# A hybrid encoder step: which queue issues the weight loads of the time mixing layer

## The chip, the cores and the metric

The kernel runs on one core of a Trainium2 chip. The metric is the device time of one execution in microseconds; the table below gives the median of the runs of the kernel before. Durations of single instructions, waits and transfers come from one profiled execution, whose own time stands beside its span. Names: PE is TensorE, PEld its weight loads, DVE VectorE, ACT ScalarE, POOL GpSimd, SP SyncE. SP, ACT and POOL can issue transfers (DMAs); an engine works through its own list of instructions in order, so an issue that has to wait holds all that stands behind it in that list.

## The reference

One step of an encoder with two layers and a width of 1024, for a prompt of 1024 rows and 8 samples of 16 rows. Layer 0 is an RWKV-7 time mixing and an FFN, layer 1 an attention over a band of chunks with shared keys and values, and an FFN. Every sub-layer is normalised and modulated by shift, scale and gate that come from a condition vector. Cut to what the change touches:

```python
mod = silu(c) @ w_ada[l] + b_ada[l]          # shift, scale, gate
h = rms_norm(x, norm_mix) * (1 + sc_m) + sh_m
xx = h_prev - h
xr, xw, xk, xv, xa, xg = (h + xx * mix[i] for i in range(6))
r, k, v = xr @ w_r, xk @ w_k, xv @ w_v
decay = exp(-exp(-softplus(-(w0 + tanh(xw @ w1) @ w2)) - 0.5))
a_gate = sigmoid(a0 + (xa @ a1) @ a2)
g = sigmoid(xg @ g1) @ g2
kk = l2_normalize(heads(k * k_k))
k = k * (1.0 + (a_gate - 1.0) * k_a)
y, state = wkv7_scan(r, decay, k, v, -kk, kk * a_gate, state)
out = (group_norm(y) + bonus(r, k, v)) * g @ w_o
x = x + gt_m * out
...                                          # FFN 0, keys/values, attention, FFN 1
```

All of it is float32. A product is worked out as three products of rounded halves: each weight is split into hi and lo (`split`: ACT copies hi in a rounded form, DVE subtracts to get lo), and PE runs hi x hi, hi x lo and lo x hi.

## The kernel before

The program has two parts. `layer0a` is the time mixing of layer 0; it ends near 1320 us. Behind it stand the FFN of layer 0, the shared keys and values, the attention and the second FFN, which end the program and which the change does not touch.

`layer0a` works on three blocks of 384 columns (`NB`, `TB`). `proj(b)` makes the projections of block b: normalisation (`proj_h`), the low-rank paths for decay, a and g (`proj_lora`, with `lora_weights`, `lora_in`, `lora_pairs` and an inner function `outputs`), then k (`proj_k`), r (`proj_r`) beside small inverses, and v. `windows` runs the recurrence over chunks of 128 columns, with many round trips through DRAM: tiles are written (`spill`, `save`, names sp_... and sf_...) and read back in another layout (rr<-sf_cs, ag<-sf_a, XL, BK, pa, yg). `outproj(b)` multiplies by w_o and adds to x. The code alternates the windows of block b-1 with the projections of block b; the windows of the last block alternate with `outproj(0)`, with units 4 to 11 of the modulation (`ada_steps`) and with `outproj(1)`; `outproj(2)` comes last, alone. From `tail_open` on there are two raw buffers for weights and one load of look-ahead in `ada_steps` (`fetch_ahead`); before that there are three raw buffers.

A weight unit is 128 x 1024 float32, 512 KB. `wunit` (L253) takes a raw buffer, loads it on SP (L256) and splits it into whi (ACT, L263) and wlo (DVE, L264). The modulation's weights are loaded on SP in `ada_steps` (L203) and used without a split; the low-rank weights in `lora_weights` (L378), `lora_pairs` (L412) and `outputs` (L605). The first sixteen modulation loads, for units 0 to 3, are made while `proj_h(0)` runs; nearly all other transfers of the first part are SP's too, a few are ACT's.

`proj_k` has two small jobs on POOL: for each strip it sets the first column of each group of the tile ext to one (L703), ACT fills the rest with exponentials (L704), and POOL copies the last column of each group into eend (L705), 32 of each in all. POOL has nothing else to do before the tail of the first part, where it forms the sums x<-x (L1257) of the FFN that follows.

The order on each engine is not written by hand. The framework takes the program's text, simulates it with costs for every instruction and orders each engine's list by that simulation (`schedule_with_timeline_sim=True`), so that a job on another engine can change the order on all of them. Completion of a transfer issued on SP or ACT is told by one of eight semaphores that are used in turn; POOL's transfers have eight of their own.

Of the kernel before, what the change touches and what calls it, by code (L numbers as in the profile page):

```python
# [141 lines left out]
class Trunk:  # L142
# [54 lines left out]
    def ada_steps(self, units, tag="aux", bufs=1, tile=None):  # L197

        nc = self.nc

        def load(u, i):
            w = (tile or self.rawtile)()
            nc.sync.dma_start(w[:, :1024], self.a["wada"][u, i])  # L203
            return w
        todo = [(u, i) for u in units for i in range(4)]
        ahead = None
        for u in units:
            ps = self.bank(tag, bufs)
            for i in range(4):
                w = ahead or load(*todo.pop(0))  # L210
                ahead = load(*todo.pop(0)) if todo and self.fetch_ahead else None
                c = slice(i // 2 * 256, i // 2 * 256 + 256)
                for q in range(4):
                    mm(nc, ps[32 * q:32 * q + 32, c], self.scT[:, i % 2 * 4 + q, :], w[:, q * 256:q * 256 + 256], i % 2 == 0, i % 2 == 1)
                if i < 3:
                    yield
            sb = (tile or self.rawtile)()[:, :512]
            nc.scalar.activation(sb, ps, AF.Copy)
            for j in range(4):
                mm(nc, ps[:, j * 16:(j + 1) * 16], sb[:, j * 128:(j + 1) * 128], self.C("qs"), True, True)  # L220
            pv = ps[:, 0:64].rearrange("p (j n) -> p j n", n=16)[:, :, 0:9]
            bo = PAR["bada"] + u * 4
            bv = self.par[:, bo:bo + 4].rearrange("p (j o) -> p j o", o=1).broadcast_to([128, 4, 9])
            nc.vector.tensor_tensor(self.mod[:, u * 4:u * 4 + 4, :], pv, bv, ALU.add)
            yield
# [24 lines left out]
    def halves(self, src):  # L250
        return [self.half(src[:, p * 512:(p + 1) * 512]) for p in range(2)]

    def wunit(self, wp, src, n=1024, rows=128):  # L253

        raw = self.rawtile()
        self.nc.sync.dma_start(raw[:rows, :n], src)  # L256
        hi = wp.tile([128, 1024], F32R, tag="whi", name=self.nm("whi"), bufs=self.nhi)
        lo = wp.tile([128, 1024], F32R, tag="wlo", name=self.nm("wlo"), bufs=self.nlo)
        self.split(hi[:rows, :n], lo[:rows, :n], raw[:rows, :n])
        return hi, lo  # L260
# [111 lines left out]
    def lora_weights(self, n):  # L372

        nc = self.nc
        mixes, w = self.LORA[n]
        c = 8 * w * len(mixes)
        raw, m = self.rawtile(), self.rawtile()
        nc.sync.dma_start(raw[:, :c], self.a[n])  # L378
        for j, i in enumerate(mixes):
            v = lambda t: t[:, :c].rearrange("p (k j w) -> p j k w", j=len(mixes), w=w)[:, j]  # L380
            nc.vector.tensor_tensor(v(m), v(raw), self.P(f"mix{i}").rearrange("p (k o) -> p k o", o=1).broadcast_to([128, 8, w]),
                                    ALU.mult)
        nc.vector.tensor_tensor(raw[:, :c], raw[:, :c], m[:, :c], ALU.subtract)
        self.lw[n] = []
        for t in (raw, m):
            dt = self.dp.tile([128, c], F32, name=self.nm("lw"))
            nc.scalar.dma_start(dt, t[:, :c])
            self.lw[n].append(dt)
        return raw, m
# [16 lines left out]
    def lora_pairs(self, n, c):  # L406

        if n in self.lw:
            raws = []
            for d in self.lw[n]:  # L410
                raws.append(self.rawtile())
                self.nc.sync.dma_start(raws[-1][:, :c], d)  # L412
        else:
            raws = self.lora_weights(n)
        W = []
# [97 lines left out]
    def proj(self, b):  # L513

        if b == 0:
            self.lw = {}
            ring = (f() for _ in range(2) for f in self.early)
            self.ada = self.ada_steps((0, 2, 1, 3), "acc", 2, lambda: next(ring))
            self.A0 = [self.cp.tile([128, 9], F32, name=f"A0_{f}") for f in range(8)]
            self.proj_h(0)  # L520
            self.x = self.hsplit()
            self.ada = self.ada_steps(range(4, 12))
        x, k = self.x, self.mixed(2, b)
# [39 lines left out]
    def proj_lora(self, b, hi, lo):  # L563
# [38 lines left out]

        def outputs(u, h, l, t):
            raw = self.rawtile()
            nc.sync.dma_start(raw, self.a["g2"][u])  # L605
            gh = pp.tile([128, 1024], F32R, tag="whi", name=self.nm("whi"), bufs=self.nhi)
            gl = pp.tile([128, 1024], F32R, tag="wlo", name=self.nm("wlo"), bufs=self.nlo)
            nc.scalar.activation(gh, raw, AF.Copy)
# [79 lines left out]
    def proj_k(self, b, hi, lo):  # L688
# [3 lines left out]
        for f in range(8):  # L692
# [7 lines left out]
            ext = self.pp.tile([128, 408], F32, tag="ext", name=self.nm("ext"), bufs=1)  # L700
            for s, sx, n, i in self.spans(b):
                ev = ext[:, sx].rearrange("p (g t) -> p g t", t=n + 1)
                nc.gpsimd.memset(ev[:, :, 0:1], 1.0)  # L703
                nc.scalar.activation(ev[:, :, 1:], iv[:, s].rearrange("p (g t) -> p g t", t=n), AF.Exp, scale=-KAPPA)  # L704
                nc.gpsimd.tensor_copy(self.eend[:, f, i:i + ev.shape[1]], ev[:, :, n])  # L705
            nc.scalar.activation(iv, iv, AF.Exp, scale=KAPPA)
            sq = self.ev("sq", self.nsq)
            kk = self.ev("kk")
# [465 lines left out]
    def layer0a(self, ctx):  # L1174
# [22 lines left out]
        cw.close()  # L1197
        for _ in self.outproj(2):
            pass
        ct.push(c1)  # L1200
        return ct.close

# [739 lines left out]
```

## Time and profile before

| what | value |
|---|---|
| median of 3 runs | 3872.93 us (3872.54 to 3875.93) |
| the profiled execution | 3860.7 us, span 3858.9 us |
| granted TensorE clock, mean | 0.939 of full speed |
| busy: PE, PEld | 3511.3 us (91%), 3098.6 us (80%) |
| busy: DVE, ACT, POOL | 2288.8 us (59%), 1570.8 us (41%), 570.9 us (15%) |
| moved by DMA | 552.31 MB, mean 143 GB/s |
| transfers issued on POOL | none in the trace |

How to read it: the span goes from the first instruction to the last. In the chain of work, each piece was released by the piece before it, so that its pieces add up to the span. A row of waits names who waited, for whom, the sum in us, the count and the longest. "SPq" is the list in which SP issues transfers; a transfer's name is destination<-source, with in_ for the program's inputs, and raw for the buffer of a weight unit. Numbers behind the names are left out in the profile's groups.

### The profile page before, as it was taken

How to read it: one execution, taken by the hardware profiler on the slowest of the kernel's cores; microseconds unless marked ns; L12 is line 12 of the kernel's file. 1: busy time of each engine (PE TensorE's matmuls, PEld its weight loads, DVE VectorE, ACT ScalarE, POOL GpSimd, SP SyncE). 2: the span in 40 equal slices, each digit the busy share in tenths (PEclk: the TensorE clock that was granted, in tenths of full speed). 3: DMA queues.
4: the chain of work that ended last, by engine and by line, in shares of the span. 5: the costliest groups of instructions: out<-in, count | busy, mean ns of one | idle time of the engine just before them, and what ended most of it. 6: DMA issues, size and time to landing. Idle time of an engine off the chain costs nothing.

```text
span 3858.9 us, 72261 instructions
## 1 busy us (share of the span) xinstructions
PE 3511.3 (91%) x28614; PEld 3098.6 (80%) x28614; DVE 2288.8 (59%) x4388; ACT 1570.8 (41%) x2966; POOL 570.9 (15%) x473
## 2 busy tenths in 40 slices
PE   5789899988899699999999899789889799999999
PEld 4677777777667589999887879677677699999998
DVE  4667666765445665555456742676775764554567
ACT  5555555544323433333311353565654533333310
POOL 0000000000000264454000100000000254554000
PEclk9887999898889789999999999899999899999999
DMA  5775676676765322222755113454555322222521
GB/s 207 232 230 167 196 214 174 180 217 182 202 195 165 132 73 75 76 72 95 270 179 183 70 60 99 137 149 145 147 189 174 119 77 77 72 75 93 170 86 69
DMA packets 429443, 552.31 MB, mean 143 GB/s; under 512 B 128432, under 2 KB 297520, under 8 KB 424624
## 3 DMA queue, kind: packets, MB, share of 16 engines
q1 hardware_dynamic: 374960, 528.80, 43.2%
q10 hardware_dynamic: 54144, 18.89, 2.2%
q8 instruction: 225, 3.69, 0.4%
q14 instruction: 114, 0.93, 0.1%
HBM read 413.42 MB, written 134.12 MB: 142 GB/s over the span
## 4 chain that ended last, share of the span: by engine, by line
PE 69%; DMA 9%; DVE 7%; ACT 5%; issue 2%; SPq 0%; POOL 0%; ACTq 0%; DVEq 0%; POOLq 0%
PE S L139 32%; PE PT L139 15%; PE acc L139 11%; PE st L139 3%; PE O L139 2%; PE G L139 2%; DVE h L264 1%; PE PT L1768 1%; PE aux L139 1%; DMA yg<-y 1%; PE Y L139 1%; ACT pts L1769 1%; DMA rr<-sf_cs 1%; DMA TT<-Z 1%; DMA raw<-in_wada 1%
## 5 line engine op out<-in xcount | busy, mean ns | idle before, releaser
L139 PE MATMUL S<-h,w 128*128 128x320 f32 (+1 forms) x4944 | 696.5, 299 | 20.6 <-DVE h L264 8.5
L139 PEld LDWEIGHTS S<-h,w 128*128 128x128 f32 x4944 | 674.6, 192 | 28.8 <-DVE h L264 13.5
L139 PE MATMUL acc<-mx,whi 128*128 128x384 f32 x1728 | 504.6, 370 | 56.1 <-ACT mx L263 18.3
L139 PE MATMUL S<-h,wh 128*128 128x320 f32 (+1 forms) x2844 | 527.5, 336 | 12.4 <-DVE h L1141 6.7
L139 PEld LDWEIGHTS S<-h,wh 128*128 128x128 f32 x2844 | 453.8, 188 | 67.8 <-issue 11.4
L139 PEld LDWEIGHTS acc<-mx,whi 128*128 128x128 f32 x1728 | 337.4, 204 | 87.2 <-ACT whi L263 21.6
L263 ACT ACTIVATE w<-rq 128x512 fp32r<-128x512 f32 x308 | 192.2, 629 | 501.7 <-PE S L139 201.8
L264 DVE TENSOR_TENSOR w<-rq,w 128x512 fp32r<-128x512 f32 x308 | 270.9, 883 | 201.2 <-ACT w L263 200.3
L139 PE MATMUL PT<-h,w 128*128 128x320 f32 (+1 forms) x2448 | 353.5, 299 | 15.0 <-ACT w L263 6.8
L139 PEld LDWEIGHTS PT<-h,w 128*128 128x128 f32 x2448 | 336.1, 191 | 18.5 <-ACT w L263 7.1
L139 PE MATMUL acc<-mx,wlo 128*128 128x384 f32 x864 | 316.2, 366 | 4.0 <-DVE wlo L264 4.0
L139 PE MATMUL PT<-h,wh 128*128 128x320 f32 (+1 forms) x1428 | 287.2, 344 | 11.2 <-DVE wh L264 3.9
L1327 POOL TENSOR_TENSOR t<-t,t 128x576 f32<-128x576 f32 (+1 forms) x132 | 215.1, 1630 | 415.7 <-ACT t L1334 292.8
L139 PEld LDWEIGHTS PT<-h,wh 128*128 128x128 f32 x1428 | 233.9, 190 | 42.5 <-issue 5.0
L264 DVE TENSOR_TENSOR wlo<-raw,whi 128x1024 fp32r<-128x1024 f32 x114 | 138.9, 1220 | 111.6 <-ACT whi L263 108.5
L139 PEld LDWEIGHTS acc<-mx,wlo 128*128 128x128 f32 x864 | 175.6, 203 | 13.3 <-DVE wlo L264 6.0
L263 ACT ACTIVATE whi<-raw 128x1024 fp32r<-128x1024 f32 x114 | 119.6, 1053 | 144.7 <-PE acc L139 79.4
L264 DVE TENSOR_TENSOR h<-h,h 128x1024 fp32r<-128x1024 f32 (+4 forms) x112 | 122.9, 1111 | 92.2 <-ACT h L263 75.7
L263 ACT ACTIVATE wh<-rq 128x512 fp32r<-128x512 f32 x124 | 74.8, 625 | 242.5 <-PE S L139 159.7
L263 ACT ACTIVATE h<-h 128x1024 fp32r<-128x1024 f32 (+4 forms) x112 | 103.2, 935 | 172.4 <-DMA h<-sd 112.2
L1327 DVE TENSOR_TENSOR t<-S,t 128x576 f32<-128x576 f32 (+1 forms) x116 | 86.4, 744 | 129.8 <-PE S L139 129.8
L1394 DVE TENSOR_TENSOR h<-h,S 128x640 f32<-128x640 f32 (+1 forms) x150 | 111.9, 750 | 78.8 <-PE S L139 78.6
(423 smaller groups left out, 5633.2 us busy)
## 6 DMA issues: line engine op xcount, KB each, us to landing
h<-in_wada SPq DMA_DIRECT2D x64, 512.0 KB, 6.4
rq<-in_wg SPq DMA_DIRECT2D x88, 256.0 KB, 2.6
rq<-in_wu SPq DMA_DIRECT2D x88, 256.0 KB, 2.6
rq<-in_wd SPq DMA_DIRECT2D x88, 256.0 KB, 2.9
raw<-in_wada SPq DMA_DIRECT2D x32, 512.0 KB, 4.3
kc<-in_ck SPq DMA_DIRECT2D x16, 1024.0 KB, 5.1
vc<-in_cv SPq DMA_DIRECT2D x16, 1024.0 KB, 7.3
sd<-t SPq DMA_DIRECT2D x88, 160.0 KB, 1.9
```

The source lines that it names most:

```text
L139: return nc.tensor.matmul(out, lhsT, rhs, start=start, stop=stop)
L263: self.nc.scalar.activation(hi, x, AF.Copy)
L264: self.nc.vector.tensor_tensor(lo, x, hi, ALU.subtract)
L1327: eng.tensor_tensor(out, x, y, ALU.add)
L1394: nc.vector.tensor_tensor(y, y, d, ALU.add)
L1768: nc.tensor.transpose(pt[:, j * 128:(j + 1) * 128], P[:, j * 128:(j + 1) * 128], self.C("ident"))
L1769: nc.scalar.activation(pts[:, 0:nk * 128], pt[:, 0:nk * 128], AF.Copy)
```

## The change

The change adds an attribute `wqueue` and a method `wload`. Where `wqueue` is None, `wload` issues on SP, as before; otherwise on the engine that it names. The five places named above use it. `wqueue` is set to GpSimd right after `proj_h(0)`, in the first block, and back to None behind `outproj(2)`. By this place, all 155 weight loads of the first part after the first sixteen are issued on POOL: the low-rank weights, w_k, w_r and w_v of all three blocks, modulation units 4 to 11 and w_o. Their number and buffers stay. The two small jobs of `proj_k` leave POOL: the memset goes to DVE, the copy of the last column to ACT.

```diff
--- before.py
+++ after.py
@@ -200,7 +200,7 @@
 
         def load(u, i):
             w = (tile or self.rawtile)()
-            nc.sync.dma_start(w[:, :1024], self.a["wada"][u, i])
+            self.wload(w[:, :1024], self.a["wada"][u, i])
             return w
         todo = [(u, i) for u in units for i in range(4)]
         ahead = None
@@ -250,10 +250,15 @@
     def halves(self, src):
         return [self.half(src[:, p * 512:(p + 1) * 512]) for p in range(2)]
 
+    wqueue = None
+
+    def wload(self, out, src):
+        (self.wqueue or self.nc.sync).dma_start(out, src)
+
     def wunit(self, wp, src, n=1024, rows=128):
 
         raw = self.rawtile()
-        self.nc.sync.dma_start(raw[:rows, :n], src)
+        self.wload(raw[:rows, :n], src)
         hi = wp.tile([128, 1024], F32R, tag="whi", name=self.nm("whi"), bufs=self.nhi)
         lo = wp.tile([128, 1024], F32R, tag="wlo", name=self.nm("wlo"), bufs=self.nlo)
         self.split(hi[:rows, :n], lo[:rows, :n], raw[:rows, :n])
@@ -375,7 +380,7 @@
         mixes, w = self.LORA[n]
         c = 8 * w * len(mixes)
         raw, m = self.rawtile(), self.rawtile()
-        nc.sync.dma_start(raw[:, :c], self.a[n])
+        self.wload(raw[:, :c], self.a[n])
         for j, i in enumerate(mixes):
             v = lambda t: t[:, :c].rearrange("p (k j w) -> p j k w", j=len(mixes), w=w)[:, j]
             nc.vector.tensor_tensor(v(m), v(raw), self.P(f"mix{i}").rearrange("p (k o) -> p k o", o=1).broadcast_to([128, 8, w]),
@@ -409,7 +414,7 @@
             raws = []
             for d in self.lw[n]:
                 raws.append(self.rawtile())
-                self.nc.sync.dma_start(raws[-1][:, :c], d)
+                self.wload(raws[-1][:, :c], d)
         else:
             raws = self.lora_weights(n)
         W = []
@@ -518,6 +523,7 @@
             self.ada = self.ada_steps((0, 2, 1, 3), "acc", 2, lambda: next(ring))
             self.A0 = [self.cp.tile([128, 9], F32, name=f"A0_{f}") for f in range(8)]
             self.proj_h(0)
+            self.wqueue = self.nc.gpsimd
             self.x = self.hsplit()
             self.ada = self.ada_steps(range(4, 12))
         x, k = self.x, self.mixed(2, b)
@@ -602,7 +608,7 @@
 
         def outputs(u, h, l, t):
             raw = self.rawtile()
-            nc.sync.dma_start(raw, self.a["g2"][u])
+            self.wload(raw, self.a["g2"][u])
             gh = pp.tile([128, 1024], F32R, tag="whi", name=self.nm("whi"), bufs=self.nhi)
             gl = pp.tile([128, 1024], F32R, tag="wlo", name=self.nm("wlo"), bufs=self.nlo)
             nc.scalar.activation(gh, raw, AF.Copy)
@@ -700,9 +706,9 @@
             ext = self.pp.tile([128, 408], F32, tag="ext", name=self.nm("ext"), bufs=1)
             for s, sx, n, i in self.spans(b):
                 ev = ext[:, sx].rearrange("p (g t) -> p g t", t=n + 1)
-                nc.gpsimd.memset(ev[:, :, 0:1], 1.0)
+                nc.vector.memset(ev[:, :, 0:1], 1.0)
                 nc.scalar.activation(ev[:, :, 1:], iv[:, s].rearrange("p (g t) -> p g t", t=n), AF.Exp, scale=-KAPPA)
-                nc.gpsimd.tensor_copy(self.eend[:, f, i:i + ev.shape[1]], ev[:, :, n])
+                nc.scalar.activation(self.eend[:, f, i:i + ev.shape[1]], ev[:, :, n], AF.Copy)
             nc.scalar.activation(iv, iv, AF.Exp, scale=KAPPA)
             sq = self.ev("sq", self.nsq)
             kk = self.ev("kk")
@@ -1197,6 +1203,7 @@
         cw.close()
         for _ in self.outproj(2):
             pass
+        self.wqueue = None
         ct.push(c1)
         return ct.close
 
```

What this does to the lists of the engines shows best at two places. The first is the start. ACT's list of before, from the copy BKT<-acc of a modulation unit on; lw are the prepared low-rank weights that are stored for the other blocks, raw_429 and raw_430 the two halves of wa1, whi their rounded parts, XL the copy of a modulation unit's sums for which PE waits:

```order
L218 ACTIVATE BKT_212<-acc_187 128x512
L331 ACT_TABLE_LOAD
L331 ACTIVATE rstd_178<-rstd_178 128x408
L332 ACTIVATE ntmp_180<-rstd_178 128x408
L387 DMA lw_437<-raw_430 128x1024
L387 DMA lw_435<-raw_429 128x1024
L263 ACTIVATE whi_439<-raw_429 128x1024
L263 ACTIVATE whi_443<-raw_430 128x1024
L1017 ACTIVATE UV_3279<-S_136 64x256
L1018 ACTIVATE UV_3279<-S_136 64x256
L218 ACTIVATE XL_244<-acc_219 128x512
```

ACT's list of the change from its fourth row on, where nacc and ntmp are the squares of hb, the first block's input:

```order
L174 ACTIVATE scT<-scT 128x256
L392 DMA lw_437<-raw_430 128x1024
L392 DMA lw_435<-raw_429 128x1024
L268 ACTIVATE whi_439<-raw_429 128x1024
L268 ACTIVATE whi_443<-raw_430 128x1024
L435 ACTIVATE nacc_153<-hb 128x408
L435 ACTIVATE ntmp_155<-hb 128x408
```

The stores and splits of wa1 have moved from behind the normalisation to ahead of it; XL now follows the stores of the next low-rank weight, g1a, and the two copies UV. On DVE the preparation of wa1 moves in the same way, ahead of the sums of the squares.

The second place is the tail, where `outproj(2)` loads its eight units of w_o; raw_13623 is the fifth, raw_13746 the eighth. SP's list of before (x<-e stores the block's result, rr<-in_x reloads x):

```order
L1169 DMA x_108<-e_2260_13493 128x384
L1166 DMA rr_13572<-in_x 128x384
L256 DMA raw_13623<-in_rw_o 128x1024
L1169 DMA x_108<-e_2267_13533 128x384
L1166 DMA rr_13613<-in_x 128x384
L256 DMA raw_13664<-in_rw_o 128x1024
L256 DMA raw_13705<-in_rw_o 128x1024
L1169 DMA x_108<-e_2274_13574 128x384
L1166 DMA rr_13654<-in_x 128x384
L256 DMA raw_13746<-in_rw_o 128x1024
```

POOL's list of the change from the fourth load of the same eight on; the TENSOR_TENSOR rows are the sums for the FFN:

```order
L256 DMA raw_13582<-in_rw_o 128x1024
L1264 ISA
L1264 TENSOR_TENSOR x_13812<-x_13812,x_13808 128x256
L1264 TENSOR_TENSOR x_13813<-x_13813,x_13809 128x256
L1264 TENSOR_TENSOR x_13808<-x_13808 128x256
L1264 TENSOR_TENSOR x_13809<-x_13809 128x256
L1264 TENSOR_TENSOR x_13808<-x_13808,x_13812 128x256
L256 DMA raw_13623<-in_rw_o 128x1024
L1264 TENSOR_TENSOR x_13809<-x_13809,x_13813 128x256
L1264 TENSOR_TENSOR x_13812<-x_13812,x_13808 128x256
L256 DMA raw_13664<-in_rw_o 128x1024
```

The fifth load has moved from SP, where it stood between stores and reloads, to behind five sums on POOL, and the sixth behind two more; the last two follow after the nine sums that come then. The stores and reloads on SP no longer stand behind loads that wait for a buffer.

## The prediction

> **What bounds the kernel now.** I read the page's chain first, to see who holds the end, then busy time by stages, then the waits of SP, ACT and PE inside the stage that the change touches. The last section of chain on the page, and the stages (columns: stretch, its length, busy us of PE, PEld, DVE, ACT and POOL with instruction counts, granted clock, DMA share, GB/s):
>
> ```profile
> PE 69%; DMA 9%; DVE 7%; ACT 5%; issue 2%; SPq 0%; POOL 0%; ACTq 0%; DVEq 0%; POOLq 0%
> ...
> 100.00:700.00 600.00, 525.00 (x5363) 442.82 (x5361) 404.01 (x860) 329.37 (x612) 6.26 (x35) 0.88 0.70 202
> ...
> 930.00:1190.00 260.00, 227.36 (x2463) 175.20 (x2463) 125.99 (x293) 79.80 (x149) 0.00 (x0) 0.86 0.71 199
> ...
> 1400.00:3859.00 2459.00, 2331.37 (x16805) 2130.80 (x16803) 1432.71 (x2583) 912.88 (x1730) 495.97 (x351) 0.98 0.36 117
> ```
>
> PE is the bound. From 1400 us on it works 2331 of 2459 us, and none of that code is touched, so the change can only move the point at which that part starts. In the first 1400 us PE is still busy 87% of the time (525.00 of 600, 227.36 of 260). What is to be had is the rest, 75 us in one stretch and 33 in the other, and it is shared by many short waits. POOL is empty there. SP, which issues nearly every transfer, is not: its longest waits between 60 and 1340 us (what waits, for whom: us in total, times, longest) and, from the same view, ACT's and PE's waits for transfers are
>
> ```profile
> SPq L256 <- DVE wlo L264: 144.3, 38, 23.0
> ...
> ACT rr L552 <- DMA rr<-sf_cs: 42.0, 18, 5.6
> ACT mx L263 <- DMA mr<-yg: 27.2, 11, 7.6
> ACT whi L263 <- DMA raw<-in_rw_o: 24.7, 6, 7.3
> ACT kp L713 <- DMA ag<-sf_a: 22.1, 11, 6.0
> ...
> PE aux L139 <- DMA raw<-in_wada: 7.5, 6, 2.0
> ```
>
> The first row is the case for the change: 38 times SP stood with a weight load whose raw buffer was still read by DVE's split, 144.3 us in all, and everything behind that load on SP stood too. The rows under it say who could profit and who could lose. The reloads (sf_cs, yg, sf_a) stay on SP and could come earlier; the weight loads that are themselves waited for (in_rw_o, in_wada) go to the new queue.
>
> **Part 1: what SP gets back.** A hold of SP costs only if what stands behind it is awaited. The chain has SPq at 0%, that is under half a per cent, 19.3 us of 3858.9. The three kinds of reload were awaited for 42.0 + 27.2 + 22.1 = 91.3 us in 40 waits, 2.3 us each, while one of them takes longer than that only to land (columns: KB, median us from issue to landing):
>
> ```profile
> raw<-in_rw_k SPq DMA_DIRECT2D x24, 512.0 KB, 3.9
> raw<-in_rw_r SPq DMA_DIRECT2D x24, 512.0 KB, 5.4
> ...
> rr<-sf_cs SPq DMA_DIRECT2D x48, 192.0 KB, 3.4
> ...
> ag<-sf_a SPq DMA_DIRECT2D x24, 192.0 KB, 2.9
> ...
> gl<-sp_g SPq DMA_DIRECT2D x18, 256.0 KB, 4.0
> ...
> yg<-y ACTq DMA_DIRECT2D x18, 256.0 KB, 4.7
> ```
>
> So most of a wait is flight (2.9 to 3.4 us), and the queue is the smaller part. SP's issue of a weight load lasts 0.33 us by its row in part 3, with the step to the next issue 0.42 (1281.79 to 1282.21). If one weight load stood ahead of half of the 40 reloads, 20 x 0.4 = **-8 us**. The ends: nothing, if the transfers that matter were ready late anyway; and -27 us, if the whole 19.3 us of SPq on the chain goes as well. I take -8, since the quoted chain has SPq at 0% and a reload's flight stays. The 155 weight loads also stop using the eight semaphores that SP's and ACT's transfers share in turn; I count that inside the -8.
>
> **Part 2: loads that are awaited.** The transfers of weights on the chain between 930 and 1190 us (start, us, what):
>
> ```profile
> 967.25 5.54 DMA raw<-in_rw_v
> 1005.25 6.38 DMA raw<-in_wada
> 1048.59 6.34 DMA raw<-in_rw_o
> 1065.97 5.40 DMA raw<-in_wada
> 1072.34 5.46 DMA raw<-in_wada
> 1113.64 4.38 DMA raw<-in_wada
> 1145.58 5.63 DMA raw<-in_rw_o
> ```
>
> Seven loads, 39.1 us. There are two raw buffers in this stage and one load of look-ahead, and each of these steps begins with a buffer coming free, not with SP coming free: no step of the chain that names SPq stands between. What POOL adds to such a load in time to issue or land, the end gets in full. The trace has no transfer issued on POOL at all, so I bound it. The low end is 0. The nearest row of another queue is the 256 KB yg<-y on ACT's, 4.7 us against 4.0 for the 256 KB gl<-sp_g on SP's: +0.7. [...] I take the nearest row: 7 x 0.7 = **+5 us**, range 0 to +17. In the blocks' first two thirds there are three raw buffers and loads run ahead, so there I count nothing; the six in_rw_o waits of ACT and six in_wada waits of PE above are all that the loads had.
>
> [...]
>
> **Part 3: the start and the tail.** The change sets the queue already after the first block's normalisation, so the first block's LoRA weights go to POOL too, which is free from the beginning. Now (start, us, engine, line, [idle before]):
>
> ```profile
> 14.93 0.54 ACT L430 ACTIVATE nacc<-hb 128x408 f32<-128x408 f32 x1 [8.71 <-DMA hb<-in_xg]
> ...
> 17.48 0.33 SPq L378 DMA_DIRECT2D raw<-in_wa  x1
> ...
> 36.43 2.00 ACT L263 ACTIVATE whi<-raw 128x1024 fp32r<-128x1024 f32 x2 [8.59 <-DVE raw L383]
> 37.52 2.36 DVE L264 TENSOR_TENSOR wlo<-raw,whi 128x1024 fp32r<-128x1024 f32 x2 [1.50 <-ACT whi L263]
> ...
> 39.19 0.60 ACT L218 ACTIVATE XL<-acc 128x512 f32<-128x512 f32 x1
> ...
> 39.84 1.89 PE L139 MATMUL acc<-cst,XL 128*128 128x16 f32 x8 [6.61 <-ACT XL L218]
> ```
>
> ACT stood 8.59 us for DVE's preparation of the raw wa1, and PE 6.61 us for the copy XL that ACT has behind it. In the changed order the two whi and wlo stand ahead of the squares of hb, in time in which ACT was idle (8.71 us before 14.93). XL then comes after two 0.4 us copies alone. Of the 6.61 us I take **-4**: the g1a preparation (two DVE operations) moves ahead of hb's scaling and takes about 2.4 us of it back, worked out from twice the 1.2 us that one of its kind takes in the 2.36 row. Ends: -6.6, and +6 if the first POOL load lands so late that the squares, now behind it on ACT, start after 14.93 us.
>
> In the tail POOL has work of its own, the Strassen sums of the next stage:
>
> ```profile
> 1281.79 0.33 SPq L256 DMA_DIRECT2D raw<-in_rw_o  x1
> 1282.21 0.38 SPq L1169 DMA_DIRECT2D x<-e  x1
> ...
> 1283.15 18.43 SPq L256 DMA_DIRECT2D raw<-in_rw_o  x2
> ...
> 1279.62 7.30 POOL L1257 TENSOR_TENSOR x<-x,x 128x256 f32<-128x256 f32 x2 [465.96 <-DVE h L264]
> 1286.88 1.43 POOL L1257 TENSOR_TENSOR x<-x 128x256 f32<-128x256 f32 x2
> 1288.27 5.43 POOL L1257 TENSOR_TENSOR x<-x,x 128x256 f32<-128x256 f32 x6
> ```
>
> The load of 1281.79 stands in the new order behind five of these sums, so it goes out when the fifth ends, some 0.9 us (5.43 / 6) after 1288.3: about 1289.2, 7.4 us later than now, and lands about 1293.6 instead of 1286.2. Now the pair behind it is split no sooner than PE wants it; the next row of the chain that names weights is the split of a later load:
>
> ```profile
> 1300.02 1.22 DVE wlo L264
> 1301.28 19.45 PE acc L139 x94
> ```
>
> So of 7.4 us later at most a part is seen. The same reordering frees SP, which stood 18.43 us over two loads. I take **+3**, from 0 to +7.4.
>
> **Part 4: the small jobs.** On POOL (min/median/max ns) they were
>
> ```profile
> L703 POOL MEMSET ext<- x32: 104/108/114, 1.7 to 811.0; 128x6 f32 x16, 128x4 f32 x8, 128x8 f32 x8
> ...
> L705 POOL COPY eend<-ext x32: 185/190/1533, 117.7 to 813.1; 128x6 f32<-128x6 f32 x16, 128x4 f32<-128x4 f32 x8, 128x8 f32<-128x8 f32 x8
> ...
> L918 ACT ACTIVATE p<-st 32x256 f32<-32x256 f32 x32 | 12.0, 375 | 14.0 <-PE st L139 13.3
> ```
>
> 32 memsets on DVE at about POOL's 0.11 us are 3.5 us of an engine that is two thirds busy; 32 copies on ACT, at most 375 ns each, are 12 us of one that is 55% busy (329.37 of 600). Each stands between two exponentials of the same strip. The slack of ACT hides most; I take a quarter, **+3**. Ends: 0 and +12.
>
> **The sum.** -8 + 5 - 4 + 3 + 3 = -1 us. The profiled execution took 3860.7 us, so 3859.7 in its terms. The median of the runs shown, 3872.93, is 12.2 us above it, and I carry the difference to it: **3872 us**. A measurement of this kernel can tell about 0.2% from no change, 7.7 us. The reordering of every engine's list, which follows from other queues and costs in the scheduler, has no term; I allow +-10 us for it, a tenth of the 108 us in which PE is idle in the two stretches above.
>
> **Rivals.** (a) **SP's holds matter more.** If the awaited reloads also lose the 19.3 us that the chain may have in SPq, part 1 is -27 and the sum -20: 3853 us. For it speaks the 144.3 us row; against it SPq 0%. Chance 0.34. (b) **The loads themselves are late**, which is slower. [...] It decides from about +1.9 us a load, since (7.7 + 1) / 7 = 1.2 above the 0.7 taken. [...] Chance 0.2. [...] (c) **The first POOL load is late at the start**: the +6 end of part 3 instead of -4, 3882 us. Chance 0.08. (d) **Nothing to see** is my forecast itself: gain and loss within 7.7 us, chance 0.38. The change touches more than it says (the first block too), so that it does nothing is no case.
>
> **How the numbers follow.** Of the forecast's 0.38, the reordering lets 0.02 fall on either side; of (a)'s 0.34 a tenth stays within 0.2%. That gives faster 0.36, same 0.37, slower 0.27. The range takes in (a) with half of the reordering, 3853 - 5 = 3848, and (b), 3892, with 2 us more: 3848 to 3894. The likeliest case's own range is 3865 to 3880.
>
> **What would show it.** Right: the SPq row with 144.3 us is gone; PE's 6.61 us before 39.84 has shrunk to some 2; the seven chain rows of weights are each 0.5 to 1 us longer. Part 1 is wrong if the 91.3 us of ACT's waits fall by more than 20 us, or rise. Part 2 is wrong if weights on the chain take 7 us or more, or if they appear before 900 us. The tail is wrong if PE's long run at 1301.28 starts over 7 us later against the stretch before it. The forecast falls if PE's idle time before 1400 us changes by more than 8 us.

## The result, and the profile after

The changed kernel takes 3900.53 us in the median (3896.77 to 3907.33) against 3873.03 us before (3872.54 to 3875.93): a ratio of 1.0057 on record, with a 95% interval of 1.0039 to 1.0075. It is slower: by 0.57%, 22 us, by that ratio, and by 27.5 us between the two medians. Run again beside other kernels it gave 1.0058 (1.0036 to 1.0080). The prediction, 3872 us with a range up to 3894, missed it.

The profiled execution took 3896.77 us. To see where the time went, each execution is cut where PE has done the same matrix work: at the start of the first block's k units, at the end of its v units, at the start of the w_o stage (outproj(0), modulation units 4 to 11, outproj(1)), at the end of outproj(2). Stage rows of before, cut there (columns as in the prediction's stage rows), and then of the changed kernel:

```profile
137.40:302.90 165.50, 136.43 (x1145) 118.97 (x1144) 110.23 (x224) 93.02 (x172) 2.50 (x12) 0.91 0.80 234
302.90:923.70 620.80, 560.20 (x6540) 464.97 (x6539) 411.07 (x902) 327.76 (x633) 9.17 (x49) 0.88 0.66 189
923.70:1316.00 392.30, 326.27 (x3325) 256.61 (x3322) 208.52 (x458) 130.71 (x247) 19.54 (x16) 0.85 0.62 180
1316.00:3858.90 2542.90, 2398.33 (x17173) 2190.24 (x17172) 1490.34 (x2684) 950.54 (x1802) 537.54 (x384) 0.97 0.35 117
```

```profile
135.30:319.00 183.70, 141.16 (x1173) 125.22 (x1174) 112.34 (x233) 91.34 (x174) 11.62 (x22) 0.85 0.74 216
319.00:941.60 622.60, 568.91 (x6532) 477.96 (x6520) 411.18 (x921) 332.32 (x661) 33.77 (x65) 0.85 0.66 187
941.60:1347.40 405.80, 336.40 (x3321) 260.60 (x3319) 210.14 (x459) 131.40 (x246) 48.95 (x72) 0.83 0.59 174
1347.40:3895.00 2547.60, 2407.20 (x17173) 2197.43 (x17172) 1495.33 (x2684) 949.27 (x1801) 541.97 (x384) 0.97 0.35 116
```

The first block's projections take 183.70 us for 165.50, the w_o stage 405.80 for 392.30. The long middle, where the loads have slack, takes 622.60 for 620.80, though all its loads have moved too. The rest differs by less than two profiles of one kernel do, as shown below. So there are two places, +18 and +13.5 us, and PE loses its time in them in two ways. In the first, PE's idle time grows by 13.5 us (165.50 - 136.43 = 29.1 to 183.70 - 141.16 = 42.5). In the second it grows by 3.4 us only (66.0 to 69.4); the other 10.1 us are PE being busy longer (326.27 to 336.40) on the same matrix work, at a granted clock of 0.83 for 0.85.

SP's second longest wait of before, then SP's longest waits between 60 and 1380 us in the changed kernel, and ACT's waits for w_o and for the three kinds of reload that the prediction added up:

```profile
SPq L1169 <- DVE e L1141: 31.7, 12, 5.8
```

```profile
SPq L1175 <- DVE e L1147: 87.7, 14, 17.8
SPq L545 <- ACT kp L604: 61.8, 12, 40.9
SPq L822 <- PE G L852: 43.6, 6, 15.5
SPq L1175 <- DVE e L1152: 43.4, 8, 19.5
SPq L545 <- DVE kp L724: 40.8, 10, 10.2
...
ACT rr L558 <- DMA rr<-sf_cs: 44.0, 17, 5.2
ACT mx L268 <- DMA mr<-yg: 39.7, 12, 8.7
ACT whi L268 <- DMA raw<-in_rw_o: 32.1, 7, 7.6
...
ACT kp L719 <- DMA ag<-sf_a: 23.0, 11, 5.6
```

The row of 144.3 us is gone, as the change means it to. In its place SP stands at stores: x<-e (L1175) 87.7 us where it was 31.7 (L1169), the save of kp (L545) 61.8 and 40.8. All of SP's waits together, from the first block's k units to the end of outproj(2), are 757 us before and 834 in the changed kernel. ACT's waits for the three kinds of reload sum to 44.0 + 39.7 + 23.0 = 106.7 us; they were 91.3. When both kernels were profiled again (before_again and after_again below), SP's waits were 758 and 828 us, and those for the reloads 92.5 and 91.5, the last from these rows:

```profile
ACT mx L268 <- DMA mr<-yg: 39.8, 13, 8.6
ACT rr L558 <- DMA rr<-sf_cs: 36.3, 15, 6.1
ACT whi L268 <- DMA raw<-in_rw_o: 32.8, 7, 7.4
...
ACT kp L719 <- DMA ag<-sf_a: 15.4, 7, 6.0
```

So SP stands longer than before, in both pairs of profiles, and the waits for reloads do not fall; whether they rise, two profiles do not tell.

At the start, POOL, ACT and PE read:

```profile
1.72 0.69 POOL L256 DMA_DIRECT2D raw<-in_wa  x1
...
11.91 7.17 ACTq L392 DMA_DIRECT2D lw<-raw  x2
19.12 2.00 ACT L268 ACTIVATE whi<-raw 128x1024 fp32r<-128x1024 f32 x2 [13.21 <-DMA YL<-in_wada]
21.04 0.53 ACT L435 ACTIVATE nacc<-hb 128x408 f32<-128x408 f32 x1
...
39.65 1.06 PE L139 MATMUL acc<-cst,XL 128*128 128x16 f32 x8 [2.18 <-ACT XL L218]
```

PE's wait for XL has shrunk from 6.61 to 2.18 us, but the matmul starts at 39.65 instead of 39.84: the store of wa1 held ACT's list for 7.17 us, and the squares of hb began at 21.04 instead of 14.93.

### The profile page after: what moved, and what is told of

It reads as the page before. It is cut to its first block, busy times and chain, and to the rows that moved or that the text cites. A ratio compares the mean times of both kernels' runs of the same rounds, so it can differ in the third digit from the quotient of the medians.

```text
span 3895.0 us, 72310 instructions
## 1 busy us (share of the span) xinstructions
PE 3540.6 (91%) x28614; PEld 3125.9 (80%) x28614; DVE 2297.2 (59%) x4420; ACT 1572.7 (40%) x2998; POOL 645.1 (17%) x564
## 3 DMA queue, kind: packets, MB, share of 16 engines
q0 software_dynamic: 21840, 79.31, 6.7%
## 4 chain that ended last, share of the span: by engine, by line
PE 70%; DMA 11%; DVE 9%; issue 5%; ACT 4%; SPq 1%; POOL 0%; ACTq 0%; DVEq 0%; POOLq 0%
PE S L139 32%; PE PT L139 15%; PE acc L139 13%; PE st L139 3%; PE O L139 2%; DVE h L269 1%; PE G L139 1%; PE PT L1775 1%; PE aux L139 1%; DMA sp_b<-ag 1%; DMA raw<-in_rw_o 1%; DMA h<-out_kT 1%; DMA yg<-y 1%; DMA rr<-sf_cs 1%; DMA BK<-sp_k 1%
## 5 line engine op out<-in xcount | busy, mean ns | idle before, releaser
L139 PE MATMUL acc<-mx,whi 128*128 128x384 f32 x1728 | 512.5, 376 | 68.5 <-ACT mx L268 22.1
L139 PE MATMUL S<-h,wh 128*128 128x320 f32 (+1 forms) x2844 | 528.4, 337 | 12.6 <-DVE h L1147 7.1
```

The source lines that it names most:

```text
L139: return nc.tensor.matmul(out, lhsT, rhs, start=start, stop=stop)
```

## Experiments

All ratios are against executions of the kernel before that ran beside the kernel tried. Theories: **Q**, a load freed from SP's list competes with the transfers that are awaited; **J**, the small jobs cost; **R**, any new order moves the time by chance.

**small_only, loads_only, from_block1, to_outproj.** The first is the kernel before with these two lines, the others are the changed kernel with one edit each.

```diff
 # small_only, in before
-                nc.gpsimd.memset(ev[:, :, 0:1], 1.0)
+                nc.vector.memset(ev[:, :, 0:1], 1.0)
-                nc.gpsimd.tensor_copy(self.eend[:, f, i:i + ev.shape[1]], ev[:, :, n])
+                nc.scalar.activation(self.eend[:, f, i:i + ev.shape[1]], ev[:, :, n], AF.Copy)
 # loads_only, in the changed kernel: the same two lines back
 # from_block1, in proj
-            self.wqueue = self.nc.gpsimd
+        if b == 1:
+            self.wqueue = self.nc.gpsimd
 # to_outproj, in layer0a
+        self.wqueue = None
         self.tail_open(ct)
```

> Only the two small jobs of proj_k leave POOL; every weight load stays on SP. Theory Q (queue: a weight load issued on POOL goes out as soon as its buffer is free, shares the 16 transfer engines with the stores and reloads that the next step awaits, PE idles, and the clock is halved for the window that follows): no change, within 6 us of before. Theory J (the memset and the copy now stand in proj_k's chain on DVE and ACT, which is where the changed kernel loses its first 14 us, between 137 and 222 us): 10 to 16 us slower than before. Theory R (any new order of the lists moves the PE's idle windows and so the clock, by some 15 us either way): anywhere from 15 us faster to 15 us slower.

> All 155 loads on POOL as in the changed kernel, but the memset and the copy stay on POOL, between the loads. Theory Q: as slow as the changed kernel, 3890 to 3910 us, since the loads still run beside SP's transfers. Theory J: 14 us faster than the changed kernel, about 3886, unless the loads wait behind the small jobs, which wait for DVE and ACT. Theory R: no relation to the two, 3860 to 3910.

> The changed kernel with the queue set only when the second block's projections begin: the first block's loads stay on SP, the small jobs stay on DVE and ACT. Theory Q: the 14 us lost between 137 and 222 us come back, the 13 us lost between 1080 and 1145 us stay: 3883 to 3890. Theory J: nothing comes back, 3895 to 3905. Theory R: no relation, 3860 to 3910.

> The changed kernel with SP issuing again from the stage with two raw buffers on (w_o and the modulation units 4 to 11). Theory Q: the 13 us lost between 1080 and 1145 us come back, the first 14 stay: 3884 to 3890, and the weights on the chain there take as long as before, 4.4 to 6.4 us. Theory J: the same, since the small jobs end at 813 us and leave this stage alone; it differs from Q in the first stage alone. Theory R: no relation, 3860 to 3910.

Measured: small_only 1.000 (0.998 to 1.002), loads_only 1.0105 (1.0076 to 1.0133), from_block1 1.0084 (1.0057 to 1.0111), to_outproj 0.9987 (0.9971 to 1.0004). The w_o stage lasts 395.10, 417.80, 411.00 and 382.50 us. Taking POOL out of that stage alone brings the whole loss back, though it also leaves the stage 10 us shorter than in before, where the same queue loads it; taking it out of the first block brings nothing, against Q's 14 us. The two places of the changed kernel are told apart by the first block's row: small_only and loads_only read

```profile
134.80:308.30 173.50, 138.41 (x1177) 120.36 (x1179) 110.70 (x230) 91.03 (x172) 0.00 (x0) 0.87 0.78 227
```

```profile
133.10:311.20 178.10, 138.86 (x1171) 122.20 (x1173) 110.46 (x224) 91.84 (x169) 14.25 (x33) 0.87 0.75 222
```

Of 165.50 us before, the small jobs alone make 173.50 and the loads alone 178.10, both 183.70. PE is idle there for 35.1 us with the jobs alone (173.50 - 138.41) and 29.1 before. The other profiles of this section sort this place further. Three profiles with neither the jobs nor the first block's loads moved have 165.50 to 166.40 us for it; five with the jobs moved and these loads and all stores on SP (small_only, from_block1, block12, outproj_only, outproj_act) 173.50 to 179.60; five with both moved (the change, after_again, to_outproj, block0_only, after_x1pool) 177.60 to 185.20. So the jobs take the larger part here, 8 to 14 us, and the loads some 7 more on average. Yet small_only as a whole is no slower, to within 0.2% or 8 us, so that this stage's loss does not show in full in its total. J falls as a price of the whole kernel: loads_only, with the jobs back on POOL, is slower than the change, not faster.

**outproj_only, block12, block0_only, before_again.** POOL in one stage each, in the changed kernel; and the kernel before once more.

```diff
 # outproj_only: not set in proj, but in layer0a
+        self.wqueue = self.nc.gpsimd
         self.tail_open(ct)
 # block12: from_block1 and to_outproj together
 # block0_only, in proj
+        if b == 1:
+            self.wqueue = None
         x, k = self.x, self.mixed(2, b)
```

> Loads on POOL only in the stage with two raw buffers (w_o and modulation units 4 to 11, 56 loads); the three blocks' projections load on SP; small jobs on DVE and ACT. Theory B (the loss is made in this stage, where loads are awaited and w_o and the modulation share two buffers and now one POOL list): 15 to 35 us slower than before, with the stretch from the first w_o load to the last outproj(1) step 10 to 25 us longer. Theory A (the loss is made in the projections, by loads that compete with stores): within 6 us of before. Theory R (each new order lands at random within 15 us): no relation.

> Loads on POOL in the second and third blocks' projections alone (w_k, w_r, w_v and the stored low-rank weights of two blocks); first block and the stage of w_o on SP. Theory B: within 8 us of before, either way. Theory A: 15 to 30 us slower than before, since from_block1, which shares this part, was the furthest behind when that stage began. Theory R: no relation.

> Loads on POOL in the first block alone, up to the end of its low-rank part and of its k, r and v units (the queue goes back to SP when the second block's projections begin). Theory B: within 8 us of before. Theory A: the 14 us lost between 137 and 222 us show in full, 10 to 16 us slower. Theory R: no relation.

> The kernel before itself, once more, with its own profile: what two profiles of the same lists differ by. All theories: a ratio of 1.000. If the number of half-clock windows before 1400 us is fixed by the order of the lists it stays near 127; if it is chance it may come out anywhere up to the 152 of the changed kernel.

Measured: 1.0011 (0.9994 to 1.0029), 1.0023 (1.0010 to 1.0037), 1.0045 (1.0029 to 1.0060) and 0.9994 (0.9979 to 1.0009). The three parts do not add up to the whole (0.11 + 0.23 + 0.45 = 0.79%, and block12 with block0, which is to_outproj, is -0.13% where its parts add up to +0.68%): the order of the lists matters by as much as the effect that is looked for, as R says, though R alone does not give the stage lengths. before_again is the ruler. Its PE row and two of its stages:

```profile
PE 3538.2 (91%) x28614; PEld 3123.2 (81%) x28614; DVE 2290.3 (59%) x4388; ACT 1571.6 (41%) x2966; POOL 570.2 (15%) x473
...
138.90:305.30 166.40, 136.09 (x1147) 118.40 (x1145) 110.24 (x224) 92.94 (x172) 2.50 (x12) 0.91 0.79 232
...
932.10:1324.80 392.70, 329.16 (x3323) 258.82 (x3321) 208.62 (x458) 130.79 (x247) 19.54 (x16) 0.84 0.62 180
1324.80:3874.60 2549.80, 2407.96 (x17173) 2199.13 (x17172) 1491.17 (x2684) 951.34 (x1802) 537.35 (x384) 0.97 0.36 116
```

The same lists gave a span of 3874.6 us instead of 3858.9, with PE busy 26.9 us longer (3538.2 to 3511.3) on the same 28614 matmuls, at a lower granted clock. So of the 36 us between the first two profiles (3895.0 - 3858.9) some 16 are chance of the clock; the two stages in question repeat within 1 us (166.40, 392.70).

**both_dve, after_x1pool, stores_pool, after_stores.** Theory **S** was made from SP's new stands: reloads ready to go stand behind stores. The standing in sum that the expectations give counts from the last rise of a reload's own semaphores; a trace does not say which rise a reload waits for, so SP's own waits are used here instead. **T**: loads on a ring of their own (the changed kernel's page has 79.31 MB on a queue q0 that the page of before does not list) slow the transfers they meet.

```diff
 # both_dve: small_only, with the copy on DVE
+                nc.vector.tensor_copy(self.eend[:, f, i:i + ev.shape[1]], ev[:, :, n])
 # after_x1pool, in outproj of the changed kernel
-            nc.sync.dma_start(self.x1[:, f, cols], o)
+            nc.gpsimd.dma_start(self.x1[:, f, cols], o)
 # stores_pool: small_only with this line, spill, save, the two stores of v and wkv_s so
 # after_stores: the changed kernel with the same five
```

> The kernel before with both small jobs on DVE; all loads on SP. A new order of the lists with nothing of the queues changed. Theory R (chance of the order): up to 15 us either way. Theories S and T below: within 6 us of before; projections (up to the start of the w_o stage) 924 to 937 us long, w_o stage 382 to 399 us, reloads standing ready in SP's list for about 450 us in sum in the first and about 220 us in the second, as in the other kernels that load on SP.

> The changed kernel with the 24 stores x<-e of the out-projections on POOL as well. Theory S (SP does not stand less: where it stood at weight loads it now stands at stores whose data come late, 60 us at x<-e in the w_o stage, and the window reloads behind them start late): the w_o stage shrinks from 406 to 385 to 398 us, the reloads' standing in it from 428 to about 250 us, and the kernel is 8 to 20 us faster than the changed one. Theory T (the weights' transfers, on a ring of their own, slow the reloads and stores they meet, and are themselves awaited): nothing is gained, 395 to 415 us for the stage; the stores make it rather worse, since they stand behind weight loads on POOL.

> The reverse split: weights and reloads on SP, the projections' and out-projections' stores (spill, save, v, the sample state, x<-e) on POOL; small jobs on DVE and ACT. Theory S: SP no longer stands at stores, so the reloads' standing falls below the 450 and 220 us of before, unless the weight loads take its place; 0 to 20 us faster than before. Theory T: no weights compete from another ring, so as before; the stores' issue on POOL costs about what it costs on SP: within 8 us. Slower by over 8 us speaks against both, and for a cost of POOL's transfers as such.

> Weights and the same stores on POOL, reloads alone on SP. Theory S: reloads stand least of all, but POOL's list now mixes loads that wait for buffers with stores that wait for data: the loads stand at stores instead, 0 to 25 us slower than the changed kernel. Theory T: as slow as the changed kernel, 10 to 30 us slower than before.

Measured: 1.0060 (1.0039 to 1.0082), 1.0062 (1.0035 to 1.0089), 0.9994 (0.9972 to 1.0015), 1.0049 (1.0029 to 1.0070). S falls as a price. With the stores x<-e off SP's list, the w_o stage of after_x1pool lasted 415.50 us instead of 405.80, and SP stood as long at the next item, the reload of x (L1172):

```profile
SPq L1172 <- DVE e L1147: 91.6, 14, 16.9
```

In stores_pool all of SP's waits came to 900 us, more than in the changed kernel, and the projections ended at 919.1 us, earlier than before; but its w_o stage lasted 409.00 us, with every weight load on SP. So a stage of over 400 us is not a mark of loads on POOL alone. both_dve was meant to be neutral and was not: the copy on DVE waits for ACT's exponentials, and holds DVE's list.

```profile
DVE eend L705 <- ACT ext L704: 15.5, 8, 7.5
```

Its 0.6% are therefore no clean measure of R.

**outproj_act, stores_proj, after_again.** ACT's queue instead of POOL's for the w_o stage (theory **G**: it is POOL's way of issuing); on POOL the stores of the projections alone; the changed kernel again.

```diff
 # outproj_act, in outproj_only
-        self.wqueue = self.nc.gpsimd
+        self.wqueue = self.nc.scalar
 # stores_proj: small_only with spill, save and the two stores of v on gpsimd
```

> As outproj_only, but the 56 loads of the w_o stage go out on ACT's queue instead of POOL's. Theory T (what costs is that 512 KB loads run on a ring of their own beside the reloads, whichever engine issues them): reloads in that stage land in 4.4 us or more on average (4.1 to 4.3 where SP issues the loads, 4.4 to 4.8 where POOL does), the stage stays at 400 us or more, apart from what ACT loses by standing at buffers. Theory G (it is POOL's way of issuing, 0.53 us each and later landing): reloads land in 4.1 to 4.3 us as on SP; the weights in 4.5 to 4.9.

> Weights on SP; on POOL only the stores of the projections (spill, save, v), none in the w_o stage; small jobs on DVE and ACT. Stores on POOL gave the shortest projections (919 us), SP alone the shorter w_o stages (382 to 399). Theory T and G alike: the two add, 919 + 392, so 5 to 15 us faster than before. If order alone decides (R), no relation: 15 us either way.

> The changed kernel again, with a profile of its own, on the chip of the others. All theories: a ratio of 1.004 to 1.008. Under T and G the two stages repeat, 940 to 950 and 400 to 412 us, with reloads of the second landing in 4.6 to 4.9 us; under R too, since the lists are the same, so this run only gives the scatter of one list from execution to execution.

Measured: 1.0021 (1.0006 to 1.0036), 0.9980 (0.9962 to 0.9999), 1.0058 (1.0036 to 1.0080). With ACT issuing, SP's reloads of the w_o stage (those whose landing the trace tells) land in 4.26 us on average. They took 4.17 and 4.34 us in the two profiles of before, and 4.0 to 4.4 in eight profiles of kernels that load there on SP; 4.54 and 4.53 in the two profiles of the changed kernel, and 4.3 to 4.7 in eight that load there on POOL. So the later landing goes with POOL, as G says, though the two ranges touch. But the stage lasts 402.70 us with ACT too, so later landing is not all of it, or ACT's own standing takes its place; this run does not tell which. The changed kernel repeats its stages:

```profile
138.70:320.70 182.00, 138.63 (x1168) 123.42 (x1169) 111.49 (x231) 91.51 (x174) 11.62 (x22) 0.86 0.74 216
...
945.70:1351.20 405.50, 339.91 (x3322) 261.90 (x3320) 210.06 (x458) 131.47 (x246) 48.96 (x72) 0.81 0.59 174
```

Against before_again the first block's row is 15.6 us longer and the w_o row 12.8; the other three stretches together are 2.2 us shorter, so that the two places make up all of the 26.2 us between these two profiles (3900.8 - 3874.6). In the w_o row PE is again idle for 2.1 us more only (63.5 to 65.6), and busy for 10.8 us more at the lower clock.

**outproj_plain, stores_proj_out.** The w_o stage's loads on POOL in two other surroundings: the kernel before, and stores_proj.

```diff
 # outproj_plain: outproj_only with the two small jobs back on gpsimd
 # stores_proj_out: outproj_only with the stores of stores_proj on gpsimd
```

> The kernel before, with the 56 loads of the w_o stage alone on POOL; small jobs stay on POOL, where they end before. The cleanest pair to before. Theory P (loads on POOL in the w_o stage cost, in whatever surroundings: three pairs so far gave +0.61, +0.70 and +0.11%): 0.2 to 0.7% slower than before, projections 924 to 932 us as before, the w_o stage 400 to 415 us against 392, its reloads landing in 4.4 to 4.8 us against 4.1. Theory R (chance of the order): no relation, 0.3% either way.

> The fastest kernel so far, stores_proj (0.998 of before), with the loads of the w_o stage on POOL. Theory P: 0.2 to 0.7% slower than stores_proj, so 0.1 to 0.5% slower than before; reloads of that stage land in 4.4 to 4.8 us against 4.2. Theory R: no relation to stores_proj, 0.3% either way of it.

Measured: 1.0046 (1.0029 to 1.0064) and 0.9973 (0.9954 to 0.9991). outproj_plain is the pair to before with the fewest lines changed: the first block's row is the same, and the w_o stage is 410.10 us long. (By the trace 48 of the stage's 56 loads moved; eight of the modulation's were still issued by SP.) But its middle stage, whose loads stay on SP, lasts 638.40 us for 620.80 and 626.80 in the two profiles of before, so that its projections end at 938.8 us instead of the 924 to 932 expected; this pair too moves more than the stage that it edits.

```profile
134.90:300.40 165.50, 135.67 (x1145) 116.68 (x1145) 110.09 (x224) 92.82 (x172) 2.53 (x12) 0.92 0.80 236
...
938.80:1348.90 410.10, 343.52 (x3324) 268.28 (x3321) 210.54 (x459) 130.65 (x247) 44.92 (x64) 0.82 0.59 173
```

What the transfers do in that stage shows in the landing times, from 924 to 1180 us in before and from 938 to 1200 us here (KB each, median us):

```profile
raw<-in_wada SPq DMA_DIRECT2D x28, 512.0 KB, 4.3
...
mr<-yg SPq DMA_DIRECT2D x16, 192.0 KB, 4.0
rr<-in_x SPq DMA_DIRECT2D x10, 192.0 KB, 4.0
...
BK<-sp_b SPq DMA_DIRECT2D x10, 128.0 KB, 4.8
```

```profile
raw<-in_wada POOLq DMA_DIRECT2D x24, 512.0 KB, 5.3
...
mr<-yg SPq DMA_DIRECT2D x16, 192.0 KB, 3.3
...
rr<-in_x SPq DMA_DIRECT2D x10, 192.0 KB, 6.0
...
BK<-sp_b SPq DMA_DIRECT2D x10, 128.0 KB, 6.0
```

The moved loads land 1.0 us later (0.6 against before_again, where this row reads 4.7). Of the transfers that never left SP, some land 1 to 2 us later, while mr<-yg lands 0.7 us earlier; the average over all of them rises by 0.2 to 0.4 us (4.52 us for 4.17 and 4.34). stores_proj_out, however, is no slower than stores_proj (0.9973 to 0.9980), with a stage of 396.30 us for 404.60. Five pairs differ in the queue of the w_o stage's loads alone, by +0.11% (outproj_only to small_only), +0.61% (from_block1 to block12), +0.70% (the change to to_outproj), +0.46% and -0.07%: 0.36% on average, 14 us, with a scatter as large. Three pairs differ in the first block's loads alone: -0.27%, -0.36% and +0.45%, none on average. Three differ in the loads of the second and third block alone: +0.73% (from_block1 to outproj_only), +0.23% (block12 to small_only) and -0.58% (to_outproj to block0_only). So by pairs no single stage's loads carry the +0.57% clear of this scatter; the w_o stage comes nearest. stores_proj_out beats both kernels, by 0.27% against before, and it is one of the kernels in which SP stands longest, 880 us in all, 147.9 of them at weight loads behind DVE's splits.

## Why the prediction was wrong, step by step

**The bound** was right: past 1400 us nothing changed, and everything was decided by when that part starts.

**Part 1, what SP gets back (-8 us)**, is the step that failed. It took for granted that SP would get its 144.3 us back, and that the 40 awaited reloads would then start earlier. Neither came: SP's waits in all rose from 757 and 758 us to 834 and 828, and ACT's waits for the three reloads went from 91.3 and 92.5 us to 106.7 and 91.5, which is no gain. The 144.3 us row went, but an in-order list stands at whatever is late next, and here that is the stores, whose data come later than SP reaches them. The sign named for this part, that the 91.3 us rise, was met in the first profile and not in the second. That SP's standing is itself the price was my next theory, and it was refuted: the fastest kernels, stores_proj and stores_proj_out, are among those in which SP stands longest (884 and 880 us).

**Part 2, the awaited loads (+5 us)** had the right sign and was mis-sized, and its mechanism is not the main one. It priced seven loads at +0.7 us each. The 150 loads of 512 KB in the first part, as far as the trace tells their landing, landed only some 0.2 us later: after 4.66 and 4.74 us on average in the two profiles of before, 4.91 and 4.96 in the two of the changed kernel. ACT's waits for w_o rose from 24.7 and 21.6 us to 32.1 and 32.8. The w_o stage lasts 13.5 and 12.8 us longer in the changed kernel, and 17.8 in outproj_plain (410.10 - 392.30). Most of that is not waiting: PE is busy 10.1 and 10.8 us longer on the same matrix work, with 41 and 44 stretches of 3.4 us at half clock in the stage where before had 35 and 36. The sum had no term for the clock. Why there are more such stretches was not settled; that shifted landings move PE's gaps is a guess, and kernels that load on SP had between 28 and 43. The weights on the chain are not each longer, as I said they would be. The changed kernel's chain has

```profile
1060.08 5.45 DMA raw<-in_rw_o
1103.14 4.67 DMA raw<-in_rw_o
1117.26 6.15 DMA raw<-in_rw_o
1134.84 4.49 DMA raw<-in_wada
1140.34 9.02 DMA raw<-in_rw_o
1168.35 4.30 DMA raw<-in_rw_o
```

six loads, 34.1 us, against seven and 39.1; one of them took 9.02 us, over the 7 that I had named as a sign against this part. Rival (b), late loads, had the direction and this place right. No run shows the +17 us at the end of this part's range, nor the 3892 us that the range takes from (b): beside the 0.2 us of later landing, POOL's issue took 527 to 537 ns in all 32 loads of the row below, and of the 56 loads that POOL issued during the stage in the changed kernel, the 24 behind whose issue DVE was busy for over 60% of the next 2 us landed after 4.73 us on average, the 19 with DVE busy for under 30% after 4.82.

```profile
L256 POOL DMA_DIRECT2D raw<-in_wada x32: 527/527/537, 885.9 to 1175.3; - x32
```

**Part 3, start (-4 us)**: the wait fell as said (6.61 to 2.18 us) and the gain was lost at once, as the squares, now behind the store of wa1 on ACT, began 6 us later. That is the event of the term's other end, +6, which I had left to rival (c), and it came together with the gain. From 0 to the first block's k units the kernel takes 135.30 us, and 138.70 when run again, for 137.40 and 138.90 before: nothing. **Tail (+3 us)**: nothing there either, as PE is idle for 24.0 us of the stage's last 60 before and for 24.6 in the changed kernel. The fifth load did go out behind POOL's sums, and the sixth behind two more:

```profile
1319.96 0.91 POOL L1264 TENSOR_TENSOR x<-x,x 128x256 f32<-128x256 f32 x1
1320.82 0.58 POOL L256 DMA_DIRECT2D raw<-in_rw_o  x1
1321.41 1.44 POOL L1264 TENSOR_TENSOR x<-x,x 128x256 f32<-128x256 f32 x2
1322.79 0.57 POOL L256 DMA_DIRECT2D raw<-in_rw_o  x1
```

**Part 4, small jobs (+3 us)**: the copy takes about 0.2 us on ACT (192 to 217 ns in small_only), half of the bound I used. The first block's projections still lengthen by 8 us or more with the jobs alone; the whole kernel does not, within 0.2%. Beside loads on POOL the jobs are better moved than left: loads_only is 0.48% slower than the change, outproj_plain 0.35% slower than outproj_only.

**The range** ended at 3894, 7 us short. Its upper end let one mechanism fail at a time, and it gave the first block's k, r and v units no term at all, since loads have slack there. That place lost 18.2 us in one pair of profiles and 15.6 in the other, 13 of them as idle time of PE, and the two moves share it: 8 us from the jobs, 12.6 from the loads, each alone. What is late in it was not settled; a single instance is the store sp_b<-ag of 135.83 us, which landed after 6.1 us when POOL's load went out 0.16 us behind it, and whose counterpart before took 2.7. How much of the +0.57% belongs to this place is open too, since the pairs for the first block's loads average to nothing. The chances were also added up wrongly: 0.9 x 0.34 + 0.02 = 0.33 for faster and 0.2 + 0.08 + 0.02 = 0.30 for slower, where the prediction has 0.36 and 0.27.

## What to carry to other kernels

A long wait in an in-order transfer list is no saving until it is known what stands behind it and what that list will stand at next. Here the list without the loads stood longer than with them. The projections' stores on POOL gave 0.9980 and 0.9973 where the loads gave 1.0057, so stores are worth trying before loads; but a gain of 0.2 to 0.3% is within what a new order does here, and stores_pool, with more stores on POOL, gave 0.9994. When a stage grows, split it into idle and busy time of the bound engine first: in the w_o stage most of the growth was the clock. And where a scheduler orders all lists, one edit is a new draw: judge it by several pairs that differ in that edit alone, not by one.

## What the runs showed of the hardware

The same lists gave PE busy times of 3511.3 and 3538.2 us in two executions. The clock records of the traces hold two values only, 1.0 and 0.5, in stretches of about 3.4 us or multiples of it; at half clock were, counted in units of 3.41 us, 139 in the first profile of before, 161 in the second, 166 and 168 in the two of the changed kernel. By its matmul records PE was busy for under 40% of 46 such stretches in the first profile of before and of 47 in that of the changed kernel, and each of them was followed by one at half clock. One profile was 16 us of span off the next of the same lists (3858.9 and 3874.6 us).

A transfer issued on POOL occupied it for 0.53 us, against medians of 0.33 to 0.40 on SP, and its 512 KB landed some 0.2 us later on average (4.66 and 4.74 us on SP, 4.91 and 4.96 on POOL, 150 loads each; in single rows, as in_wada in outproj_plain, up to 1.0). Less expected, SP's own reloads landed later beside it, by 0.2 to 0.4 us on average (4.17 and 4.34 us before, 4.54 and 4.53 in the changed kernel). Single rows scatter far more: rr<-in_x reads 4.0 us in both profiles of before, 6.0 in outproj_plain, and 4.8 and 4.5 in the changed kernel. Loads on ACT's queue left the average at 4.26 us.
